# Two-layer block on one core: the SwiGLU input products accumulate in PSUM onto half banks copied by ScalarE, one more pair of column blocks goes by seven products, and half of a gate vector is loaded later

## The chip, the cores and the metric

The kernel runs on one core of a Trainium2 chip. The metric is the device time of one execution in microseconds (us): the median of three runs of the kernel before is 1515.11 us (1514.31 to 1516.73).

## The reference

Two residual layers over 512 tokens of width 1024, all in fp32. Each layer normalizes the tokens, scales and shifts them by conditioning vectors (a SiLU of `c` times a 1024x6144 matrix per layer), applies a mixer (a gated linear recurrence in layer 0, dilated attention in layer 1), adds the result back under a gate, and then does the same with a SwiGLU feed-forward part (FFN):

```python
u = rms_norm(h, norm_g[layer, 2]) * (1.0 + sc2) + sh2
gate, up = jnp.split(u @ w_in, 2, axis=-1)        # w_in: 1024 x 5632
y = (jax.nn.silu(gate) * up) @ w_out              # w_out: 2816 x 1024
h = h + (1.0 + g2) * rms_norm(y, norm_g[layer, 3])
```

The change touches the product `u @ w_in` of both layers and the place at which half of the gate vector `g2` of layer 0 is made.

## The kernel before

**Numbers.** Every fp32 operand of a large product is split into a rounded part and a rest (`hi` and `lo`), and each product is three matmuls: hi by hi, hi by lo, lo by hi (`three`, line 437). ScalarE (ACT) makes the rounded part by a copy with a cast, VectorE (DVE) the rest by a subtraction.

**Weights.** `Stream` (line 38) walks one list of items, written down in order in lines 340 to 425. An item is a 1 MB piece of weights or of a conditioning matrix; two raw buffers hold what has been loaded, SyncE (SP) issues the loads in the order of the list, and a buffer is loaded again when its item has been worked off. `weave` (line 342) puts conditioning items between weight items at a given spacing. A conditioning item is summed on VectorE by four multiply-adds over 512 columns (line 259, its first at line 257), reduced over the partitions on GpSimd (POOL, line 261), and finished by `row_fin` (line 295: two 256 KB rows are loaded and VectorE adds and multiplies, lines 306 and 307) for a gate.

**The first product of an FFN.** `ffn` (line 907) makes 22 blocks of 128 columns for `gate` and as many for `up`. `PLAIN` (line 362) says how many groups of two gate and two up blocks are made directly: per group 4 blocks x 8 slices of the inner dimension x 3 matmuls = 96 matmuls over 512 tokens. The first group is made inside `mixer_out`. The other blocks, two per group, go through `seven_products` (line 771): a gate block and its up block over 512 tokens make a 2x2 by 2x2 block product, and seven smaller products take the place of eight. Each small product (`run`, line 835) is 4 x 3 = 12 matmuls over 256 tokens, so a pair of a gate and an up block takes 84. The left operands are quarters R (three quarters of the weights as they are) and Sm (four sums of quarters); the right operands are quarters of u (`B11`, `B21`, `B22`) and sums of them (`t1`, `t2`, `T3`, `T4`, made once per layer by `token_sums`). `B11` is a copy, shifted by 144 columns.

**The order around the change** is written out by hand (`manual_schedule`): each engine takes its instructions in the program's order. For pair `i`, `runs(i)` puts the seven products into half banks of four PSUM banks (512 fp32 columns each): the four `mm` banks for even pairs, the two `a` and two `b` banks for odd ones. Meanwhile the weights of pair `i+1` are prepared: `r_hi` (ACT, line 802) and `r_lo` (DVE, 806), one sum on GpSimd (`sum_a`, 810), two on VectorE (814, 818), two casts (ACT, 826) and two subtractions (DVE, 830). The seven results of pair `i` are added on the way out of PSUM: two ACT copies of 256 columns (lines 889, 899), VectorE adds (855, 859, 865), a GpSimd add (860), one SiLU (ACT, 866) and the last multiplication (DVE, 870). The tile framework puts the semaphores: whatever two engines do in one PSUM bank is put one after the other, by bank.

**After it**, `y = mid @ w_out` runs per 1 MB weight piece as 48 matmuls over 512 columns. The conditioning items of layer 1 are woven between these pieces.

Of the kernel before, what the change touches and what calls it, by code (L numbers as in the profile page):

```python
# [21 lines left out]
NF = DFF // P  # L22
# [15 lines left out]
class Stream:  # L38
# [120 lines left out]
def block_kernel(tc, x, c, positions, ada_w, ada_b, norm_g, hgrn_w_in, lower, hgrn_norm_g, hgrn_w_out,  # L159
# [8 lines left out]
    with ExitStack() as ctx:  # L168
# [190 lines left out]
        hg.append(win(W, 3 * D + 3 * 256))  # L359
        hg_o = [wtok(hgrn_w_out[0], kq, hf * 512) for hf in range(2) for kq in range(2)]  # L360

        PLAIN = (3, 2)

        def ffn_ws(l):

# [9 lines left out]
        items += weave(hg_o, gate_loads[1:2], 0)  # L375
        f0a, f0b = ffn_ws(0)
        n0 = 2 * PLAIN[0]
        items += weave(f0a[:n0], gate_loads[2:] + [[fin] for fin in gate_fins], 2) + f0a[n0:]
        items += weave(f0b[:9], ada_seq((1, 1), (1, 0)), 0, 0.9) + f0b[9:]
        AW = attn_w_in[0]  # L380

        def av(g, hf):
# [54 lines left out]
        def three(ps, ah, al, bh, bl, start, stop):  # L437
            pe.matmul(ps, ah, bh, start=start, stop=False)  # L438
            pe.matmul(ps, ah, bl, start=False, stop=False)  # L439
            pe.matmul(ps, al, bh, start=False, stop=stop)  # L440
# [327 lines left out]
                    dve.tensor_sub(tl[:, k], t[k], th[:, k].bitcast(F32))  # L768
            return cut

        def seven_products(fs, mid, sgp, spare, th, tl):


            fs = list(fs)
            quarter = lambda a, k: a[:, k * 512:(k + 1) * 512]
# [5 lines left out]
            for copy, t in ((act.copy, uh), (dve.tensor_copy, ul)):  # L781
                for a, b in ((112, 256), (0, 112)):
                    copy(t[:, 0:4, a + 144:b + 144], t[:, 0:4, a:b].bitcast(F32))
            B11 = [(uh[:, k, 144:400], ul[:, k, 144:400]) for k in range(4)]
# [3 lines left out]
            H2 = lambda a: a.rearrange("p (a n) -> p a n", a=2)  # L788
            ring = []
            raw, g_of = {}, {}  # L790
# [12 lines left out]

            def r_lo(i):
                hi, lo = places(i)[0]
                dve.tensor_sub(lo[:, 0:1536], raw[i][:, 512:], hi[:, 0:1536].bitcast(F32))  # L806

            def sum_a(i):
                r = Q4(raw[i])
                pool.tensor_add(r[:, 2], r[:, 2], r[:, 0])  # L810

            def sum_b(i):
                r = Q4(raw[i])
                dve.tensor_tensor(r[:, 0:2], r[:, 0:3:2], r[:, 1:2].broadcast_to((P, 2, 512)), op=OP.add)  # L814

            def sum_c(i):
                r = Q4(raw[i])
                dve.tensor_add(r[:, 3], r[:, 3], r[:, 1])

            def s_cut(i, k):  # L820
                src = Q4(raw[i])[:, 1:3] if k == 0 else Q4(raw[i])[:, 0:4:3]
                return [Q4(t)[:, 2 * k:2 * k + 2] for t in places(i)[1]] + [src]

            def s_hi(i, k):
                hi, lo, src = s_cut(i, k)
                act.copy(hi, src)  # L826
# [12 lines left out]

            def runs(i):  # L840
                R, Sm = places(i)
                b = [bank("mm") for _ in range(4)] if i % 2 == 0 else [bank(t) for t in "abab"]
                g_of[i] = b
                half = lambda n, k: b[n][:, k * 256:k * 256 + 256]
                first = [(half(0, 0), R, 0, B11), (half(3, 1), R, 512, T4), (half(1, 0), R, 1024, B21)]
                for k in (1, 2, 0) if i == 0 else range(3):
                    run(*first[k])
                run(half(1, 1), Sm, 0, t2)
                run(half(2, 1), Sm, 1024, T3)
                run(half(2, 0), Sm, 512, t1)  # L850
                run(half(3, 0), Sm, 1536, B22)

            def sums_1(i):

                dve.tensor_tensor(W[:, 0:5:4], W[:, 2:3].broadcast_to((P, 2, 256)), H2(g_of[i][1]), op=OP.add)

            def sums_2(i):

                dve.tensor_tensor(W[:, 1:6:4], W[:, 4:5].broadcast_to((P, 2, 256)), H2(g_of[i][2]), op=OP.add)
                pool.tensor_add(W[:, 3], W[:, 3], W[:, 5])  # L860

            def sums_3(i):

                if i >= 0:
                    dve.tensor_tensor(W[:, 1:3], W[:, 1:6:4], H2(g_of.pop(i)[3]), op=OP.add)
                    act.activation(W[:, 0:2], W[:, 0:2], AF.Silu)

            def finish(i):
                if i >= 0:
                    dve.scalar_tensor_tensor(H2(mid(fs[i])), W[:, 2:4], -1.0, W[:, 0:2], op0=OP.mult, op1=OP.mult)  # L870

            with tc.manual_schedule(engines=ORDERED):
                r_hi(0)
                r_lo(0)
                sum_a(0)
                sum_b(0)
                sum_c(0)
                for k in range(2):
                    s_hi(0, k)
                    s_lo(0, k)  # L880
                r_hi(1)
                for i in range(len(fs)):
# [5 lines left out]
                    finish(i - 1)  # L888
                    act.copy(W[:, 2], g_of[i][0][:, 0:256])
                    if more:  # L890
                        sum_a(i + 1)
                        sum_b(i + 1)
                        s_hi(i + 1, 0)
                        sum_c(i + 1)
                    sums_1(i)
                    if more:
                        s_lo(i + 1, 0)
                        s_hi(i + 1, 1)
                    act.copy(W[:, 3], g_of[i][2][:, 0:256])
                    if more:  # L900
                        s_lo(i + 1, 1)
                        r_hi(i + 2)
                    sums_2(i)
                sums_3(len(fs) - 1)
                finish(len(fs) - 1)

        def ffn(l, first, close, nxt, side):
            turns.close()
            close()
            with ExitStack() as fx:  # L910
# [4 lines left out]
                with ExitStack() as qx:  # L915
# [6 lines left out]
                    for j in range(PLAIN[l]):  # L922
# [990 lines left out]
```

## Time and profile before

| what | value |
|---|---|
| median of 3 runs | 1515.11 us (1514.31 to 1516.73) |
| the profiled execution, first to last instruction (span) | 1511.0 us |
| TensorE (PE) matmul busy | 1492.8 us, 99% |
| weight loads into TensorE (PEld) | 1308.2 us, 87% |
| VectorE | 1063.6 us, 70% |
| ScalarE | 720.3 us, 48% |
| GpSimd | 234.4 us, 16% |
| granted TensorE clock, mean | 0.997 |
| DMA | 199.14 MB, mean 132 GB/s |

The profile gives no time of its own for the profiled execution besides its span; the median of the timed runs stands 4.1 us above the span. The page's fifth part groups instructions by line, engine and tiles: busy us, mean ns of one, then the engine's idle time ahead of them and who ended it. In the timeline a row is: start, duration, engine, line, operation, output<-inputs, and in brackets the idle time before it and who ended it. Matmuls overlap in it, so the distance from start to start, not the duration, is what one costs.

### The profile page before, as it was taken

How to read it: one execution, taken by the hardware profiler on the slowest of the kernel's cores; microseconds unless marked ns; L12 is line 12 of the kernel's file. 1: busy time of each engine (PE TensorE's matmuls, PEld its weight loads, DVE VectorE, ACT ScalarE, POOL GpSimd, SP SyncE). 2: the span in 40 equal slices, each digit the busy share in tenths (PEclk: the TensorE clock that was granted, in tenths of full speed). 3: DMA queues.
4: the chain of work that ended last, by engine and by line, in shares of the span. 5: the costliest groups of instructions: out<-in, count | busy, mean ns of one | idle time of the engine just before them, and what ended most of it. 6: DMA issues, size and time to landing. Idle time of an engine off the chain costs nothing. (4 is left out here: it accounts for less than half of the span.)

```text
span 1511.0 us, 23542 instructions
## 1 busy us (share of the span) xinstructions
PE 1492.8 (99%) x9231; PEld 1308.2 (87%) x9231; DVE 1063.6 (70%) x1841; ACT 720.3 (48%) x1219; POOL 234.4 (16%) x208
## 2 busy tenths in 40 slices
PE   8999999999999999999999999999999999999998
PEld 6777888898999988888987888988888899999886
DVE  4587867486888896476667766686466978888633
ACT  4433443363454533375545666346655644544231
POOL 1011211031222211140001110011002212221100
PEclk9999999999999999999999999999999999999999
DMA  9654444125333366423166540365213333334521
GB/s 309 183 166 138 156 140 167 56 85 167 113 107 106 105 208 220 155 100 123 57 195 169 150 129 29 113 195 140 84 46 123 98 100 112 109 105 154 209 96 56
DMA packets 206943, 199.14 MB, mean 132 GB/s; under 512 B 6840, under 2 KB 164720, under 8 KB 206576
## 3 DMA queue, kind: packets, MB, share of 16 engines
q1 hardware_dynamic: 203856, 190.87, 40.6%
q10 hardware_dynamic: 1952, 6.65, 1.2%
q8 instruction: 72, 1.18, 0.3%
q0 software_dynamic: 1024, 0.13, 0.2%
q14 instruction: 39, 0.32, 0.1%
HBM read 192.31 MB, written 5.31 MB: 131 GB/s over the span
## 5 line engine op out<-in xcount | busy, mean ns | idle before, releaser
L89 DVE TENSOR_TENSOR lo<-raw,hi 128x2048 fp32r<-128x2048 f32 x68 | 158.8, 2337 | 91.7 <-ACT hi L88 91.7
L88 ACT CAST hi<-raw 128x2048 fp32r<-128x2048 f32 x68 | 129.7, 1908 | 190.3 <-DMA raw<-in_ffn_w_out_dram 55.2
L438 PE MATMUL ps_mm<-apart,hi 128*128 128x512 f32 x384 | 151.4, 394 | 0.0
L439 PE MATMUL ps_mm<-apart,hi 128*128 128x512 f32 x384 | 151.1, 394 | 0.0
L440 PE MATMUL ps_mm<-apart,lo 128*128 128x512 f32 x384 | 150.7, 394 | 0.1
L438 PE MATMUL ps_mm<-uh,hi 128*128 128x512 f32 (+1 forms) x400 | 146.3, 366 | 0.0
L439 PE MATMUL ps_mm<-ul,hi 128*128 128x512 f32 (+1 forms) x400 | 144.3, 361 | 1.0 <-DVE ul L538 1.0
L440 PE MATMUL ps_mm<-uh,lo 128*128 128x512 f32 (+1 forms) x400 | 144.6, 361 | 0.0
L826 ACT CAST hiq<-raw 128x1024 fp32r<-128x1024 f32 x68 | 68.1, 1048 | 64.2 <-DVE raw L814 63.4
L438 PE MATMUL ps_mm<-hi,oh 128*128 128x512 f32 x240 | 94.0, 392 | 0.0
L439 PE MATMUL ps_mm<-lo,oh 128*128 128x512 f32 x240 | 93.4, 389 | 0.0
L438 PEld LDWEIGHTS ps_mm<-uh,hi 128*128 128x128 f32 x400 | 75.5, 189 | 19.7 <-issue 8.4
L439 PEld LDWEIGHTS ps_mm<-ul,hi 128*128 128x128 f32 x400 | 75.6, 189 | 12.1 <-DVE ul L538 1.4
L440 PEld LDWEIGHTS ps_mm<-uh,lo 128*128 128x128 f32 x400 | 75.5, 189 | 11.4
L440 PEld LDWEIGHTS ps_mm<-apart,lo 128*128 128x128 f32 x384 | 72.2, 188 | 15.0 <-DVE lo L89 0.5
L439 PEld LDWEIGHTS ps_mm<-apart,hi 128*128 128x128 f32 x384 | 72.2, 188 | 14.2
L438 PEld LDWEIGHTS ps_mm<-apart,hi 128*128 128x128 f32 x384 | 72.2, 188 | 14.0
L830 DVE TENSOR_TENSOR loq<-raw,hiq 128x1024 fp32r<-128x1024 f32 x68 | 80.0, 1218 | 0.4 <-ACT hiq L826 0.4
L259 DVE SCALAR_TENSOR_TENSOR shared<-raw,cond,shared 128x512 f32<-128x512 f32 x98 | 73.3, 748 | 9.8 <-DMA raw<-in_ada_w_dram 8.8
L261 POOL PARTITION_ALL_REDUCE shared<-shared x14 | 45.9, 3278 | 200.5 <-DVE shared L259 200.5
L810 POOL TENSOR_TENSOR raw<-raw 128x512 f32<-128x512 f32 x34 | 54.7, 1609 | 101.1 <-DVE loq L806 46.3
L440 PE MATMUL ps_mm<-hi,ol 128*128 128x512 f32 x176 | 68.5, 389 | 0.0
(450 smaller groups left out, 4355.2 us busy)
## 6 DMA issues: line engine op xcount, KB each, us to landing
raw<-in_ada_w_dram SPq DMA_DIRECT2D x40, 1024.0 KB, 5.1
raw<-in_ffn_w_in_dram SPq DMA_DIRECT2D x136, 256.0 KB, 3.5
raw<-in_attn_w_in_dram SPq DMA_DIRECT2D x48, 512.0 KB, 5.1
raw<-in_ffn_w_out_dram SPq DMA_DIRECT2D x22, 1024.0 KB, 4.8
raw<-in_hgrn_w_in_dram SPq DMA_DIRECT2D x12, 1024.0 KB, 5.4
raw<-in_attn_w_in_dram SPq DMA_DIRECT2D x12, 1024.0 KB, 4.9
raw<-in_ffn_w_in_dram SPq DMA_DIRECT2D x10, 1024.0 KB, 5.0
first<-in_ada_w_dram SPq DMA_DIRECT2D x14, 512.0 KB, 7.5
```

Of the source, the lines that this page charges most:

```text
L88: self.nc.scalar.copy(hi, t)
L89: self.nc.vector.tensor_sub(lo, t, hi.bitcast(F32))
L259: dve.scalar_tensor_tensor(a, r[:, k], sc, a, op0=OP.mult, op1=OP.add)
L261: pool.partition_all_reduce(a, a, P, bass.bass_isa.ReduceOp.add)
L438: pe.matmul(ps, ah, bh, start=start, stop=False)
L439: pe.matmul(ps, ah, bl, start=False, stop=False)
L440: pe.matmul(ps, al, bh, start=False, stop=stop)
L810: pool.tensor_add(r[:, 2], r[:, 2], r[:, 0])
L826: act.copy(hi, src)
L830: dve.tensor_sub(lo, src, hi.bitcast(F32))
```

## The change

`seven_products` gets three of the four PSUM banks of the last directly made group (`seeded`) and takes one `a` and one `b` bank for itself; a bank's two halves serve even and odd pairs. Instead of adding seven results on VectorE and GpSimd, ScalarE copies a partial sum from one half bank to another inside PSUM, and the next products accumulate onto the copy:

- `first` = B11's product; a copy of it seeds `u2`; then B21's product goes onto `first`, t2's onto `u2`.
- a copy of `u2` seeds `last`; then t1's product goes onto `last`, T4's onto `u2`.
- a copy of `last` seeds `u4`, the other half of `u2`'s bank; then B22's product goes onto `last`.
- `both` = T3's product, copied to SBUF. VectorE adds it to `u2` and `u4` in one instruction and multiplies; the SiLUs of `first` and `last` are two ScalarE instructions.

The first pair uses B11 unshifted, and the shifted copy is made during it. `PLAIN` for layer 0 goes from 3 to 2. Two 1 MB loads of layer 0's `g2` matrix and the finish of that half (two 256 KB rows) go from among the input weights to among the output weights of that FFN, where the spacing of the woven items goes from 0.9 to 0.68.

```diff
-        PLAIN = (3, 2)
+        PLAIN = (2, 2)
...
-        items += weave(f0a[:n0], gate_loads[2:] + [[fin] for fin in gate_fins], 2) + f0a[n0:]
-        items += weave(f0b[:9], ada_seq((1, 1), (1, 0)), 0, 0.9) + f0b[9:]
+        items += weave(f0a[:n0], [[gate_fins[0]]], 2) + f0a[n0:]
+        items += weave(f0b[:9], gate_loads[2:] + [[gate_fins[1]]] + ada_seq((1, 1), (1, 0)), 0, 0.68) + f0b[9:]
...
+            fresh_1, fresh_x = bank("a"), bank("b")
+            class Sums:
+                def __init__(self, i):
+                    p = i % 2
+                    self.first = half(fresh_1, p)
+                    self.both = half(fresh_x, p)
+                    self.pair = seeded[p]
+                    self.u2, self.u4 = half(self.pair, 0), half(self.pair, 1)
+                    self.last = half(seeded[2], p)
...
-            def run(ps, w, o, us):
+            def run(ps, w, o, us, begin):
                 for kt in range(4):
                     a = slice(o + kt * P, o + (kt + 1) * P)
-                    three(ps, w[0][:, a], w[1][:, a], *us[kt], kt == 0, kt == 3)
...
+                    for m, (x, y) in enumerate(((0, 0), (0, 1), (1, 0))):
+                        pe.matmul(ps, w[x][:, a], us[kt][y], start=begin and kt + m == 0, stop=kt == 3 and m == 2,
+                                  skip_group_check=True)
+            def tail_a(i, s):
+                if i >= 0:
+                    act.activation(W[:, 1], s.last, AF.Silu)
+            def tail_b(i, s):
+                if i >= 0:
+                    dve.tensor_tensor(W[:, 2:4], W[:, 4 + i % 2:5 + i % 2].broadcast_to((P, 2, 256)), H2(s.pair), op=OP.add)
+            def tail_c(i):
                 if i >= 0:
                     dve.scalar_tensor_tensor(H2(mid(fs[i])), W[:, 2:4], -1.0, W[:, 0:2], op0=OP.mult, op1=OP.mult)
...
                 for i in range(len(fs)):
                     more = i + 1 < len(fs)
-                    runs(i)
-                    sums_3(i - 1)
...
+                    R, Sm = places(i)
+                    s = Sums(i)
+                    run(s.first, R, 0, B11[i > 0], True)
+                    run(s.both, Sm, 1024, T3, True)
+                    tail_a(i - 1, before)
+                    tail_b(i - 1, before)
+                    act.copy(s.u2, s.first)
+                    tail_c(i - 1)
+                    run(s.u2, Sm, 0, t2, False)
+                    run(s.first, R, 1024, B21, False)
                     if more:
                         r_lo(i + 1)
...
+                        sum_a(i + 1)
+                    act.copy(W[:, 4 + i % 2], s.both)
+                    act.copy(s.last, s.u2)
+                    if i == 0:
+                        shift()
+                    run(s.last, Sm, 512, t1, False)
+                    run(s.u2, R, 512, T4, False)
                     if more:
...
                         sum_b(i + 1)
                         s_hi(i + 1, 0)
                         sum_c(i + 1)
+                        s_hi(i + 1, 1)
                         s_lo(i + 1, 0)
+                    act.copy(s.u4, s.last)
+                    act.activation(W[:, 0], s.first, AF.Silu)
+                    run(s.last, Sm, 1536, B22, False)
                     if more:
                         s_lo(i + 1, 1)
                         r_hi(i + 2)
+                    before = s
+                tail_a(len(fs) - 1, before)
+                tail_b(len(fs) - 1, before)
+                tail_c(len(fs) - 1)
...
-                    seven_products(range(2 * PLAIN[l], NF), mid, sgp, spare, th, tl)
+                    seven_products(range(2 * PLAIN[l], NF), mid, pss, spare, th, tl)
```

More of the change, by code (lines that the diff above doesn't have):

```diff
@@ L769, in token_sums, with seven_products @@
             return cut
-        def seven_products(fs, mid, sgp, spare, th, tl):
+        def seven_products(fs, mid, seeded, spare, th, tl):
             fs = list(fs)
-            quarter = lambda a, k: a[:, k * 512:(k + 1) * 512]
             Q4 = lambda a: a.rearrange("p (s n) -> p s n", s=4)
@@ L779, in seven_products, with shift @@
             B21, B22 = u_of(1, 0), u_of(1, 1)
-            for copy, t in ((act.copy, uh), (dve.tensor_copy, ul)):
+            B11 = [u_of(0, 0), [(uh[:, k, 144:400], ul[:, k, 144:400]) for k in range(4)]]
+            def shift():
                 for a, b in ((112, 256), (0, 112)):
-                    copy(t[:, 0:4, a + 144:b + 144], t[:, 0:4, a:b].bitcast(F32))
-            B11 = [(uh[:, k, 144:400], ul[:, k, 144:400]) for k in range(4)]
+                    for copy, t in ((act.copy, uh), (dve.tensor_copy, ul)):
+                        copy(t[:, 0:4, a + 144:b + 144], t[:, 0:4, a:b].bitcast(F32))
             t1, T3, T4, t2 = (t_of(i) for i in range(4))
@@ L788, in seven_products @@
             H2 = lambda a: a.rearrange("p (a n) -> p a n", a=2)
+            half = lambda b, k: b[:, k * 256:k * 256 + 256]
             ring = []
-            raw, g_of = {}, {}
+            raw = {}
+            fresh_1, fresh_x = bank("a"), bank("b")
[7 more added lines that the diff above has]
+                    self.last = half(seeded[2], p)
             def places(i):
@@ L833, in s_lo @@
                     st.fill()
-            def run(ps, w, o, us):
+            def run(ps, w, o, us, begin):
                 for kt in range(4):
                     a = slice(o + kt * P, o + (kt + 1) * P)
-                    three(ps, w[0][:, a], w[1][:, a], *us[kt], kt == 0, kt == 3)
[L840 to L862, printed above, removed]
-                if i >= 0:
-                    dve.tensor_tensor(W[:, 1:3], W[:, 1:6:4], H2(g_of.pop(i)[3]), op=OP.add)
-                    act.activation(W[:, 0:2], W[:, 0:2], AF.Silu)
-            def finish(i):
+                    for m, (x, y) in enumerate(((0, 0), (0, 1), (1, 0))):
+                        pe.matmul(ps, w[x][:, a], us[kt][y], start=begin and kt + m == 0, stop=kt == 3 and m == 2,
+                                  skip_group_check=True)
+            def tail_a(i, s):
+                if i >= 0:
+                    act.activation(W[:, 1], s.last, AF.Silu)
[3 more added lines that the diff above has]
+            def tail_c(i):
                 if i >= 0:
@@ L881, in seven_products @@
                 r_hi(1)
+                before = None
                 for i in range(len(fs)):
                     more = i + 1 < len(fs)
-                    runs(i)
-                    sums_3(i - 1)
+                    R, Sm = places(i)
[8 more added lines that the diff above has]
+                    run(s.first, R, 1024, B21, False)
                     if more:
                         r_lo(i + 1)
-                    finish(i - 1)
-                    act.copy(W[:, 2], g_of[i][0][:, 0:256])
+                        sum_a(i + 1)
[5 more added lines that the diff above has]
+                    run(s.u2, R, 512, T4, False)
                     if more:
-                        sum_a(i + 1)
                         sum_b(i + 1)
@@ L894, in seven_products @@
                         sum_c(i + 1)
-                    sums_1(i)
-                    if more:
+                        s_hi(i + 1, 1)
                         s_lo(i + 1, 0)
-                        s_hi(i + 1, 1)
-                    act.copy(W[:, 3], g_of[i][2][:, 0:256])
+                    act.copy(s.u4, s.last)
+                    act.activation(W[:, 0], s.first, AF.Silu)
+                    run(s.last, Sm, 1536, B22, False)
                     if more:
@@ L902, in seven_products @@
                         r_hi(i + 2)
-                    sums_2(i)
-                sums_3(len(fs) - 1)
-                finish(len(fs) - 1)
+                    before = s
+                tail_a(len(fs) - 1, before)
+                tail_b(len(fs) - 1, before)
+                tail_c(len(fs) - 1)
         def ffn(l, first, close, nxt, side):
```

## The prediction

> **What bounds the kernel now.** I read the page first, for who is full.
>
> ```profile
> span 1511.0 us, 23542 instructions
> ...
> PE 1492.8 (99%) x9231; PEld 1308.2 (87%) x9231; DVE 1063.6 (70%) x1841; ACT 720.3 (48%) x1219; POOL 234.4 (16%) x208
> ...
> PEclk9999999999999999999999999999999999999999
> ```
>
> PE is busy 99% of the span at a clock that stays at nine tenths or more. Busy time of overlapping matmuls hides small pauses, so next comes the list of what PE waited for. It has eleven rows; the first, the longest, and the only one that names an FFN line:
>
> ```profile
> PE ps_mm L1140 <- DVE late L1135: 2.0, 3, 1.3
> PE ps_mm L1140 <- DVE cols L1170: 1.7, 1, 1.7
> ...
> PE ps_mm L439 <- DVE ul L538: 1.0, 2, 0.5
> ```
>
> That last row (1.0 us, a token split ahead of the FFNs) is no wait of `seven_products`: in both FFNs PE waits for nobody. So time goes only if matmuls go, and comes if PE is made to wait. The stages, by windows: two directly made groups of layer 0, its seven products, and the seven products of layer 1.
>
> ```profile
> core 0: us, PE busy (x) PEld busy (x) DVE busy (x) ACT busy (x) POOL busy (x), PEclk, DMA share, GB/s
> 338.10:381.60 43.50, 43.50 (x194) 36.03 (x193) 32.10 (x30) 15.81 (x16) 4.53 (x2) 1.00 0.48 148
> 381.60:535.40 153.80, 153.80 (x1346) 153.77 (x1345) 131.81 (x146) 73.34 (x94) 35.31 (x31) 1.00 0.40 117
> ...
> 1211.70:1384.60 172.90, 172.90 (x1513) 172.90 (x1512) 144.41 (x158) 82.63 (x106) 38.52 (x33) 1.00 0.38 111
> ```
>
> PE is full in all three, VectorE comes second (131.81 of 153.80 us), ScalarE has half its time free.
>
> **Part 1, one more group by seven products: 2.6 us less.** PE's timeline gives the steps:
>
> ```profile
> 338.08 0.40 PE L438 MATMUL ps_mm<-uh,hi 128*128 128x512 f32 x1
> ...
> 381.63 0.28 PE L438 MATMUL ps_mm<-th,spare 128*128 128x256 f32 x1
> ...
> 391.35 0.28 PE L438 MATMUL ps_a<-uh,hiq 128*128 128x256 f32 x1
> ...
> 525.75 0.28 PE L438 MATMUL ps_a<-uh,hiq 128*128 128x256 f32 x1
> ```
>
> The first row opens the second directly made group, the second ends the third: 2 groups of 96 matmuls in 43.55 us, 21.78 us each, 0.227 us a matmul. The other two are the first matmuls of pairs 1 and 15: 134.40 us for 14 pairs, 9.60 us each, 0.114 us a matmul, 1.37 us a product of 12. A group gives two pairs: 21.78 - 2 x 9.60 = **2.58 us saved**, under the 0.2% (3.0 us) that a measurement of this kernel can tell from no change.
>
> **Part 2, accumulating onto copies: PE waits once in each pair.** PE's order per pair becomes B11, T3, t2, B21, t1, T4, B22. Three of ScalarE's copies stand between a product and one that accumulates on it: `u2` (after B11's product, before t2's; T3's lies between), `last` (after t2's, before t1's; B21's between) and `u4` (after t1's, before B22's; T4's between). What such a copy takes from product to product, by rows:
>
> ```profile
> 389.88 0.28 PE L440 MATMUL ps_mm<-th,loq 128*128 128x256 f32 x1
> 389.99 0.28 PE L438 MATMUL ps_mm<-uh,hiq 128*128 128x256 f32 x1
> ...
> 390.19 0.37 ACT L899 COPY shared<-ps_mm 128x256 f32<-128x256 f32 x1 [1.82 <-PE ps_mm L440]
> ```
> ```profile
> 824.13 0.58 ACT L1809 COPY h<-ps_a 128x512 f32<-128x512 f32 x1
> 824.76 0.30 PEld L1831 LDWEIGHTS ps_b<-h,V 128*128 128x128 f32 x2 [1.77 <-ACT h L1809]
> ```
> ```profile
> 385.78 0.19 PEld L438 LDWEIGHTS ps_mm<-th,hiq 128*128 128x128 f32 x1
> ...
> 385.90 0.29 PE L438 MATMUL ps_mm<-th,hiq 128*128 128x256 f32 x1
> ```
>
> ScalarE's copy starts 0.20 us after the next product has begun (389.99 to 390.19) and takes 0.37; PE's weight load starts 0.05 us after a copy that it waited for (824.71 to 824.76); the matmul follows its weight load by 0.12. Together 0.74 us. Beneath a product of 1.37 us that is hidden, and so it is for `u2` and `last`.
>
> For `u4` it is not. `u4` is the other half of `u2`'s bank, onto which T4's product runs. In the built program this copy does not wait for t1's product: it waits for a count that PE raises only with the last matmul of T4's, because the framework keeps two engines apart by bank. B22's product waits for the copy. So the 0.74 us begin when T4's product ends, and nothing is left on PE to lie over them: the next product in PE's order is the one that waits, and behind it stands the next pair. There are 22 - 4 = 18 pairs in each layer: 36 x 0.74 = **26.6 us added**.
>
> The Trainium skill, "PSUM — Partial Sum Buffer", section "PSUM bank collisions raise a hardware error", speaks against this layout too: it says that two engines must not be in one bank over the same partitions at a time, whichever columns they use, and that PSUM is to be guarded by bank and not by address. No run so far shows such an overlap; by that rule the wait could not be made finer without moving `u4`.
>
> No trace shows ScalarE writing PSUM, so the copy's 0.37 us (PSUM to SBUF) is bounded: the hand-overs alone, 0.37 us, if the copy were free, and the 0.58 us of the row with 512 columns in its place, 0.95. I take 0.37, the row of the same shape. ScalarE's page ("ScalarE: Activation LUTs", section "What happens when an `exp` ACTIVATE runs") in the Trainium skill holds its writes to PSUM faster than those to SBUF, without a number; the sum by it would be somewhat lower.
>
> **Does another chain end later than T4's product?** Before the copy of `u4` ScalarE's order holds both casts of the next pair's sums. Their prices:
>
> ```profile
> L826 ACT CAST hiq<-raw 128x1024 fp32r<-128x1024 f32 x26 | 26.0, 1048 | 25.7 <-DVE raw L814 25.7
> L810 POOL TENSOR_TENSOR raw<-raw 128x512 f32<-128x512 f32 x13 | 21.0, 1616 | 23.1 <-DVE loq L806 12.4 <-DVE spare L806 10.7
> L814 DVE TENSOR_TENSOR raw<-raw 128x1024 f32<-128x1024 f32 x13 | 15.9, 1226 | 15.4 <-POOL raw L810 15.4
> L806 DVE TENSOR_TENSOR spare<-raw,spare 128x1536 fp32r<-128x1536 f32 x6 | 10.5, 1752 | 0.0
> ...
> L870 DVE SCALAR_TENSOR_TENSOR mid<-shared 128x512 f32<-128x512 f32 x13 | 8.9, 684 | 0.0
> ```
>
> From the end of B22's product: SiLU of `last` done at 0.20 + 0.37, last multiplication 0.68, `r_lo` 1.75, GpSimd's sum 1.62, `sum_b` 1.23, two casts 2.10: 7.95 us, some 0.2 more with hand-overs. T4's product ends six products later, at 8.23, and its copy may start at 8.43. The chain has 0.3 us to spare, so it costs nothing; were it longer than I add up, all 36 pairs would pay. VectorE loses two 0.68 us additions a pair and GpSimd one; ScalarE gains about 0.9 us (two copies, and a SiLU in two parts) in half an empty queue. The shifted copy now stands in pair 0 ahead of those casts; PE waits at `u4` there anyway: nothing. B11 unshifted in pair 0 has no row; B21 reads the same columns at 1.36 us, so nothing, at most a product more (1.37) in each layer.
>
> **Part 3, half of `g2` later: nothing.** Two 1 MB loads, two of 256 KB, 8 multiply-adds, 2 finishing steps and one GpSimd reduction leave the directly made groups, where PE was full and stays so, and go behind the first three output weight pieces, past them on SP's queue.
>
> ```profile
> L259 DVE SCALAR_TENSOR_TENSOR shared<-raw,cond,shared 128x512 f32<-128x512 f32 x98 | 73.3, 748 | 9.8 <-DMA raw<-in_ada_w_dram 8.8
> L261 POOL PARTITION_ALL_REDUCE shared<-shared x14 | 45.9, 3278 | 200.5 <-DVE shared L259 200.5
> ```
> ```profile
> 535.40:555.00 19.60, 19.60 (x89) 16.22 (x88) 19.48 (x30) 8.14 (x11) 4.49 (x2) 1.00 0.56 175
> 555.00:575.00 20.00, 20.00 (x90) 16.57 (x89) 15.64 (x36) 6.63 (x8) 3.23 (x1) 1.00 0.68 223
> ...
> 615.00:635.00 20.00, 20.00 (x90) 16.57 (x89) 5.64 (x5) 5.18 (x5) 0.00 (x0) 1.00 0.31 107
> ```
> ```profile
> 552.23 2.28 DVE L89 TENSOR_TENSOR lo<-raw,hi 128x2048 fp32r<-128x2048 f32 x1
> ```
> ```profile
> 608.43 2.29 DVE L89 TENSOR_TENSOR lo<-raw,hi 128x2048 fp32r<-128x2048 f32 x1 [2.78 <-ACT hi L88]
> ```
>
> VectorE takes 8 x 0.75 + 1.4 = 7.4 us more here, and is idle from 615. What matters is when a weight piece is split: the third piece at 554.51, the ninth at 610.72, 9.37 us apart, each with one conditioning item, so 4.7 us an item. PE uses one in 48 x 0.227 = 10.9 us and wants the ninth at 535.4 + 8 x 10.9 = 622.6: a lead of 11.9 us. Two full items and a small one come ahead of it, 9.4 to 14.1 us. So the lead just covers them, and if not, 2.2 us are lost; PE's waits in the stage before add lead (VectorE runs ahead meanwhile). I take nothing.
>
> **Sum.** 1511.0 - 2.6 + 26.6 = 1535.0 us of span. The median of the timed runs stands 4.1 us over that span; kept, that is **1539.1 us**, 1.6% slower.
>
> **The rivals.**
>
> *The copy of `u4` is hidden* (the other side). If it ran beneath T4's product, it would start after the casts, near 8.0 us, and B22's weight load is due at 8.23 - 0.12: PE would lose nothing and only part 1 is left, 1515.1 - 2.6 = 1512.5 us, within 0.2%. It decides at a hand-over of about zero after T4's product. For it: two of the three copies are hidden just so. Against: the built program's wait. Chance 0.04.
>
> *ScalarE's casts end later than T4's product.* The preparing chain (7.95 us and its hand-overs) becomes the period. Half a microsecond over 8.43 would cost 36 x 0.5 = 18 us more: 1557 us. For it: before, GpSimd's sum is what VectorE waits for (15.4 us), and VectorE what the casts wait for (25.7). Against: the sum leaves 0.3 us, and GpSimd loses its other work. Chance 0.05.
>
> *The clock drops.* A pause of 0.74 us in every 10.3 could make the granted clock give way; each tenth lost over both stages costs a tenth of 153.8 + 172.9 + 19.2 us, 35 us: 1574 us. Against it, here PE paused 1.34 us and the clock stayed at 1.00:
>
> ```profile
> 820.00:830.00 10.00, 8.54 (x48) 6.87 (x48) 9.89 (x15) 3.99 (x7) 3.73 (x2) 1.00 0.47 133
> ```
>
> Chance 0.02. The Trainium skill, "TensorE: Matmul & The Clock Gate", section "A second HAM failure mode: psum-queue depth-cycling", reports a kernel whose short pauses between groups of matmuls, while cycling PSUM banks, made the clock go up and down; the row above does not bear that out.
>
> **How the numbers follow.** The forecast has 0.87, the rivals 0.04, 0.05 and 0.02; 0.02 is left for a gain that I don't see. The range comes from the copy's price: 36 x 0.60 - 2.6 gives 1534, and 36 x 0.95 - 2.6 gives 1547; for the copy cheaper than I can bound by the nearest row I go to 1532. Slower by over 0.2%: 0.94; within 0.2%: 0.04; faster: 0.02.
>
> **What would show it.** In the changed profile: PE waits for ScalarE's copy of `u4`, 36 times, near 0.7 us each; pairs 10.3 us apart; no wait at the copies of `u2` and `last`; that copy begins 0.2 us after T4's product; ScalarE idle ahead of it, for PE; no PE wait in the output product of layer 0; clock 1.00. I am wrong if the pairs stay at 9.6 us, or if ScalarE comes to that copy late from its casts.

## The result and the profile after

The changed kernel takes 1536.16 us (median of 4 runs, 1533.8 to 1541.81) against 1514.96 us before: ratio 1.0144, 95% interval 1.0125 to 1.0164, slower. The forecast was 1539.1 us, 1532 to 1547. The profiled execution took 1536.03 us, with a span of 1534.3. Its page, the lines that answer to those of before:

```profile
span 1534.3 us, 23585 instructions
...
PE 1501.6 (98%) x9303; PEld 1313.5 (86%) x9303; DVE 1031.5 (67%) x1783; ACT 751.4 (49%) x1335; POOL 202.6 (13%) x176
...
PEclk9999999999999999999999999999999999999999
```

PE's busy time rose by 8.8 us and the span by 23.3: the rest is idle time of PE. VectorE and GpSimd have 32 us less to do each, ScalarE 31 more. The list of what PE waited for has a new first row, ahead of fourteen others. The three shown below it return later:

```profile
PE ps_mm L856 <- ACT ps_mm L909: 16.0, 36, 0.4
...
PE ps_b L1844 <- ACT h L1822: 1.1, 2, 0.8
...
PE ps_b L1853 <- ACT h L1822: 0.5, 1, 0.5
...
PE ps_mm L439 <- DVE lo L89: 0.4, 1, 0.4
```

L856 is the matmul in `run`, L909 the copy of `u4`: 36 waits, one in each pair of both layers, and none for another copy. The list gives 16.0 us, 0.45 each. PE's timeline shows that it is more. First the two first matmuls of B22's product in consecutive pairs, then the last matmul of T4's in one pair and what follows it, with the weight load and ScalarE's rows at that place:

```profile
389.22 0.39 PE L856 MATMUL ps_mm<-uh,hiq 128*128 128x256 f32 x1 [0.45 <-ACT ps_mm L909]
```
```profile
399.54 0.39 PE L856 MATMUL ps_mm<-uh,hiq 128*128 128x256 f32 x1 [0.45 <-ACT ps_mm L909]
```
```profile
429.80 0.28 PE L856 MATMUL ps_mm<-th,spare 128*128 128x256 f32 x1
430.52 0.39 PE L856 MATMUL ps_mm<-uh,hiq 128*128 128x256 f32 x1 [0.45 <-ACT ps_mm L909]
430.75 0.28 PE L856 MATMUL ps_mm<-ul,hiq 128*128 128x256 f32 x1
```
```profile
430.52 0.19 PEld L856 LDWEIGHTS ps_mm<-uh,hiq 128*128 128x128 f32 x1 [0.64 <-ACT ps_mm L909]
```
```profile
430.11 0.36 ACT L909 COPY ps_mm<-ps_mm 128x256 f32<-128x256 f32 x1 [0.66 <-PE ps_mm L856]
430.38 0.39 ACT L910 ACTIVATE shared<-ps_a 128x256 f32<-128x256 f32 x1
```

Pairs are 10.32 to 10.33 us apart, where the forecast had 9.60 + 0.74. From the last matmul of T4's product to the first of B22's are 0.72 us where 0.114 is the rule, so 0.61 is lost there. The next step is 0.23 instead of 0.114, so 0.11 more: 0.72 us a pair, and 0.725 by the distances (10.325 less 9.60). The list of waits counts from a modelled end of the last matmul (430.08) and leaves out both the restart and the part of 0.28 us that matmuls usually overlap. The distance from start to start is what counts. 36 times 0.725 is 26.1 us; less 2.6 for the direct group, 23.5, and the spans differ by 23.3.

### The profile page after: what moved, and what is told of

Read it like the earlier page. It is cut to its first block, busy times and chain, and to the rows that moved or that the text cites. A ratio compares the mean times of both kernels' runs of the same rounds, so it can differ in the third digit from the quotient of the medians.

```text
span 1534.3 us, 23585 instructions
## 1 busy us (share of the span) xinstructions
PE 1501.6 (98%) x9303; PEld 1313.5 (86%) x9303; DVE 1031.5 (67%) x1783; ACT 751.4 (49%) x1335; POOL 202.6 (13%) x176
## 5 line engine op out<-in xcount | busy, mean ns | idle before, releaser
L439 PE MATMUL ps_mm<-apart,hi 128*128 128x512 f32 x384 | 151.2, 394 | 0.0
L438 PE MATMUL ps_mm<-uh,hi 128*128 128x512 f32 (+1 forms) x368 | 133.9, 364 | 0.0
L439 PE MATMUL ps_mm<-ul,hi 128*128 128x512 f32 (+1 forms) x368 | 131.9, 358 | 1.0 <-DVE ul L538 1.0
L440 PE MATMUL ps_mm<-uh,lo 128*128 128x512 f32 (+1 forms) x368 | 132.2, 359 | 0.0
L856 PE MATMUL ps_mm<-th,hiq 128*128 128x256 f32 x360 | 99.4, 276 | 0.0
L856 PE MATMUL ps_mm<-tl,hiq 128*128 128x256 f32 x360 | 99.4, 276 | 0.0
L856 PE MATMUL ps_mm<-th,loq 128*128 128x256 f32 x360 | 99.4, 276 | 0.0
L847 DVE TENSOR_TENSOR loq<-raw,hiq 128x1024 fp32r<-128x1024 f32 x72 | 85.1, 1222 | 18.7 <-ACT hiq L843 18.7
L827 POOL TENSOR_TENSOR raw<-raw 128x512 f32<-128x512 f32 x36 | 48.2, 1339 | 356.8 <-DVE loq L823 170.6
L439 PE MATMUL ps_mm<-lo,oh 128*128 128x512 f32 x240 | 93.6, 390 | 0.4 <-DVE lo L89 0.4
L438 PEld LDWEIGHTS ps_mm<-uh,hi 128*128 128x128 f32 x368 | 69.5, 189 | 18.5 <-issue 8.4
L439 PEld LDWEIGHTS ps_mm<-apart,hi 128*128 128x128 f32 x384 | 72.2, 188 | 14.2
L439 PEld LDWEIGHTS ps_mm<-ul,hi 128*128 128x128 f32 x368 | 69.6, 189 | 10.8 <-DVE ul L538 1.4
```

The costliest lines, as they stand in the source:

```text
L856: pe.matmul(ps, w[x][:, a], us[kt][y], start=begin and kt + m == 0, stop=kt == 3 and m == 2, skip_group_check=True)
```

## The experiments

Each ratio is to the kernel before on the same chip. "Pairs" are the distances between pairs in the timeline.

**1. `u4` in a bank of its own.** The direct groups' fourth bank is free during the seven products.

```
-                    self.pair = seeded[p]
-                    self.u2, self.u4 = half(self.pair, 0), half(self.pair, 1)
+                    self.u2, self.u4 = half(seeded[p], 0), half(seeded[3], p)
...
-                    dve.tensor_tensor(W[:, 2:4], W[:, 4 + i % 2:5 + i % 2].broadcast_to((P, 2, 256)), H2(s.pair), op=OP.add)
+                    for k, u in ((2, s.u2), (3, s.u4)):
+                        dve.tensor_add(W[:, k], W[:, 4 + i % 2], u)
```

> The changed kernel with `u4` in the fourth bank that the direct groups leave free, so that no copy shares a bank with the product that runs while it is due; the addition of `both` becomes two of 256 columns. Theory (the copy of `u4` waits for T4's product because both are in one bank, and nothing covers its 0.72 us): the copy runs beneath T4's product, PE waits nowhere in the seven products, pairs 9.60 us apart, 1536.2 - 36 x 0.72 = 1510 us, at most 1513. Rival A (accumulating onto a half that ScalarE wrote costs PE by itself): the pairs stay near 10.3 us and the time near 1536. Rival B (ScalarE's casts come late to that copy): the copy starts when the casts end, not when a product ends; some 1515 to 1530, with PE waits of changing length.

Measured: 1517.79 us, ratio 1.0020 (1.0007 to 1.0033). PE's list of waits has no row of the seven products. The timeline of this kernel (its matmul line is L855; the first matmuls of two consecutive pairs, then the end of T4's and the start of B22's product, then ScalarE and B22's first weight load at that place):

```profile
439.59 0.28 PE L855 MATMUL ps_a<-uh,spare 128*128 128x256 f32 x1
```
```profile
449.19 0.28 PE L855 MATMUL ps_a<-uh,hiq 128*128 128x256 f32 x1
```
```profile
438.12 0.28 PE L855 MATMUL ps_mm<-th,loq 128*128 128x256 f32 x1
438.23 0.28 PE L855 MATMUL ps_mm<-uh,hiq 128*128 128x256 f32 x1
```
```profile
435.77 2.00 ACT L842 CAST hiq<-raw 128x1024 fp32r<-128x1024 f32 x2 [1.01 <-DVE raw L830]
437.67 0.37 ACT L909 COPY ps_mm<-ps_mm 128x256 f32<-128x256 f32 x1
```
```profile
438.12 0.19 PEld L855 LDWEIGHTS ps_mm<-uh,hiq 128*128 128x128 f32 x1
```

9.60 us a pair, 0.11 from T4's last matmul to B22's first. The bank of `u4` makes the difference between the two kinds of pairs; rival A falls. (The edit also splits one addition of VectorE into two; the second try of 2 comes to the same pairs without that.) The copy now begins beneath T4's product, when the casts end (437.67), and ends at 438.04, 0.08 us ahead of B22's weight load at 438.12. So the shared bank hid a second bound of nearly the same length, as the prediction's chain had it. The total is 5 us above the 1513 that were the most expected; see 5 and 6.

**2. The same banks in another order.** B22's product goes behind the next pair's first, T3's behind t2's, B21's behind t1's, T4's last:

```
+                    if i:
+                        run(before.last, *late, B22, False)
...
                     run(s.u2, Sm, 0, t2, False)
...
+                    if i:
+                        run(s.both, Sm, 1024, T3, True)
...
                     run(s.last, Sm, 512, t1, False)
+                    run(s.first, R, 1024, B21, False)
+                    act.copy(s.u4, s.last)
...
+                    run(s.u2, R, 512, T4, False)
```

> All banks as in the changed kernel; only the order is another: B22's product of a pair comes after the first product of the next pair, T3's after t2's, B21's after t1's, T4's last, and the copy of `u4` is issued ahead of T4's product. Each of the three copies then has a product in another bank between its source and its reader. Theory: no wait, pairs 9.60 us apart except the first of each layer (one uncovered copy, 0.7 us each), 1511 us, at most 1514. Rival A (accumulating onto copies costs by itself): near 1536. Rival C (the shared bank is bad wherever the copy stands, because it must still wait for the bank): waits move to T4's product, 1520 to 1536.

Measured: 1567.98 us, ratio 1.0334 (1.0313 to 1.0355), 11.03 us a pair: none of the theories. PE's waits, then VectorE's rows in one pair:

```profile
PE ps_a L856 <- ACT shared L914: 37.1, 32, 1.4
```
```profile
438.81 0.69 DVE L869 SCALAR_TENSOR_TENSOR mid<-shared 128x512 f32<-128x512 f32 x1 [1.82 <-ACT shared L861]
439.42 1.75 DVE L823 TENSOR_TENSOR spare<-raw,spare 128x1536 fp32r<-128x1536 f32 x1
```

No wait at `u4` is left, but another is there: the next pair's first product waits for the SiLU of `first` (L914). The `first` of two neighbouring pairs are the two halves of one bank, so this wait, too, is one by bank. With B22 a product later, the SiLU of `last` came later, VectorE's last multiplication (L869) waited 1.82 us for it, and behind that stood `r_lo` (L823), the head of the chain to the casts and that SiLU. I had moved a product without following what stands behind its readers. The second try puts `r_lo` ahead of the multiplication and the copy of `u4` between the casts:

```
                     tail_b(i - 1, before)
+                    if more:
+                        r_lo(i + 1)
+                        sum_a(i + 1)
                     act.copy(s.u2, s.first)
...
+                        s_hi(i + 1, 0)
+                        sum_c(i + 1)
+                    act.copy(s.u4, s.last)
+                    if more:
+                        s_hi(i + 1, 1)
```

> The changed kernel's banks with the order in which every copy has a product of another bank between its source and its reader, and now with VectorE's remainder `r_lo` ahead of its last multiplication, and ScalarE's copy of `u4` between the two casts, since in the first try the SiLU of `first` came 1.4 us late behind that chain and the next pair's first product waited for it. Theory: 9.60 us a pair but for the first of each layer, 1511 to 1518. If the chain is still the longer one: PE waits for that SiLU again, 10 to 11 us a pair, 1525 to 1560.

Measured: 1512.76 us, ratio 0.9997 (0.9986 to 1.0009). Pairs 9.60 us. Of the seven products only two waits are left, one in each layer's first pair:

```profile
PE ps_mm L856 <- ACT ps_mm L899: 0.9, 2, 0.4
```

So the shared bank does no harm in itself. What counts is that a product of another bank lies between the copy and its neighbours.

**3. The copy ahead of T4's product; the SiLU ahead of the copy.**

```
+                    act.copy(s.u4, s.last)
                     run(s.u2, R, 512, T4, False)
...
-                    act.copy(s.u4, s.last)
```

> The changed kernel with one line moved: the copy of `u4` is issued ahead of T4's product, directly behind t1's. Theory: the same 0.72 us of hand-over now lie between t1's product and T4's, with nothing on PE between them either; PE waits at T4's product instead of B22's, pairs 10.3 us apart, 1536 us (1534 to 1539). If it were the sharing of the bank alone that costs, whatever the order, the wait would go with the order: 1510 us.

Measured: 1546.67 us, ratio 1.0214 (1.0194 to 1.0234). The wait went to T4's product, and is as long:

```profile
PE ps_mm L856 <- ACT ps_mm L902: 17.9, 36, 0.5
```

Pairs are 10.38 to 10.49 us, up to 0.16 longer than in the changed kernel, 4 us in all; why a pause there costs a little more was not found. Of the other 6 us some 3 lie at the start of the two output products, where PE now waits for a cast (`oh`, 2.6 us by the list of waits, no such row in the changed kernel); the rest lies in the attention (6).

```
-                    act.copy(s.u4, s.last)
                     act.activation(W[:, 0], s.first, AF.Silu)
+                    act.copy(s.u4, s.last)
```

> The changed kernel with two neighbouring ScalarE lines swapped: the SiLU of `first` (0.39 us) comes ahead of the copy of `u4`. Theory: ScalarE stands idle for 0.83 us ahead of that copy, waiting for T4's product, so the SiLU fits there and nothing changes: 1536 us, within 2. Rival B (ScalarE's own chain ends late and sets the copy's start): 36 x 0.27 to 0.39 us more, 1546 to 1550.

Measured: 1544.28 us, ratio 1.0191 (1.0177 to 1.0206). By its total it speaks for rival B, by its trace it doesn't: pairs 10.34 us, against 10.33. The copy's own view, in this kernel and in the changed one, has these rows; the two after the heading tell ScalarE's idle time ahead of the copy:

```profile
its engine sat idle before it (us, times) until:
  PE ps_mm L856: 17.6, 35
```
```profile
its engine sat idle before it (us, times) until:
  PE ps_mm L856: 29.8, 36
```

The SiLU used up part of an idle time of 0.83 us, and the copy still starts when PE lets it. ScalarE's chain did not set the pause. The total's 8 us lie outside the FFNs (6).

**4. The copy done twice.**

```
                     act.copy(s.u4, s.last)
+                    act.copy(s.u4, s.last)
```

> The changed kernel with the copy of `u4` done twice, the second time writing the same numbers. Theory (whatever ScalarE does between T4's product and B22's is paid in full): ScalarE's next instruction starts 0.27 us after the copy, so each pair is 0.27 us longer, 10.60 us; 36 x 0.27 = 9.7 us more, some 1546 (1543 to 1549). If the pause were a fixed cost of the hand-over between the engines, and not of the copy: 10.33 us a pair, 1536.

Measured: 1557.66 us, ratio 1.0278 (1.0256 to 1.0300). ScalarE's rows and two starts of B22's product:

```profile
433.24 0.36 ACT L909 COPY ps_mm<-ps_mm 128x256 f32<-128x256 f32 x1 [0.67 <-PE ps_mm L856]
433.62 0.36 ACT L910 COPY ps_mm<-ps_mm 128x256 f32<-128x256 f32 x1
```
```profile
434.03 0.39 PE L856 MATMUL ps_mm<-uh,hiq 128*128 128x256 f32 x1 [0.83 <-ACT ps_mm L910]
```
```profile
444.80 0.39 PE L856 MATMUL ps_mm<-uh,hiq 128*128 128x256 f32 x1 [0.83 <-ACT ps_mm L910]
```

10.77 us a pair, 0.44 more, not 0.27: the second copy, to the same half, starts 0.39 us behind the first, where the SiLU to another place starts 0.27 behind. So ScalarE's time between T4's and B22's products is paid in full, and the price was misjudged. The list of waits has 34 of these and not 36: in the last pair of each layer the built program runs B22's product among the first matmuls of the output product, an order that the kernel does not write down. 34 x 0.44 = 15.0 us of the 21.5 over the changed kernel. The rest lies behind the seven products: PE waits at the start of both output products (`oh`, 0.98 us each), once for `lo` in the first of them (1.62 us), and longer in the attention (6).

**5. The parts taken apart.** The changed kernel again:

> The changed kernel once more, unaltered, beside the others of this set, since the parts outside the seven products differed by several us among the profiles so far. If those parts differ from execution to execution, the pairs stay 10.33 us apart and the total moves by some us: 1533 to 1543. If the first reading was typical, 1536 within 1.5.

Measured: 1536.93 us, ratio 1.0151 (1.0133 to 1.0170), pairs 10.33 us: the first reading was typical. The old products with the other two parts of the change:

```
-        PLAIN = (3, 2)
+        PLAIN = (2, 2)
...
-        items += weave(f0a[:n0], gate_loads[2:] + [[fin] for fin in gate_fins], 2) + f0a[n0:]
-        items += weave(f0b[:9], ada_seq((1, 1), (1, 0)), 0, 0.9) + f0b[9:]
+        items += weave(f0a[:n0], [[gate_fins[0]]], 2) + f0a[n0:]
+        items += weave(f0b[:9], gate_loads[2:] + [[gate_fins[1]]] + ada_seq((1, 1), (1, 0)), 0, 0.68) + f0b[9:]
```

> The products, sums and copies of the kernel before, with only the other two parts of the change: one direct group fewer in layer 0 (18 pairs there), and half of the conditioning vector's loads later. Theory (these two are worth 21.78 - 2 x 9.60 = 2.6 us and nothing else): 1512.6 us, PE waits nowhere in the FFNs but perhaps 0.4 us in layer 0's output product. Rival D (the moved loads or the missing group cost what the kernel with `u4` in its own bank lost against its forecast, some 5 us): 1516 to 1519.

Measured: 1513.33 us, ratio 0.9999 (0.9988 to 1.0011). The 2.6 us aren't in the total. The new sums with `u4` in its own bank, three direct groups and the old loads (the same lines the other way):

> `u4` in its own bank, but with three direct groups in layer 0 and the loads where they were before: only the sums of products are new. Theory (the new sums cost PE nothing once no copy is waited for; the direct group and the loads are all that is left): 9.60 us a pair, 1515.2 us, as before. Rival D: 1515 too. Rival E (the new sums, by ScalarE's or VectorE's other work, cost the 5 us that were missing): 1518 to 1521.

Measured: 1511.78 us, ratio 0.9983 (0.9974 to 0.9992), below what either theory gave. The new sums cost nothing and seem to gain 2.6 us, and not within the products, where the pairs are 9.60 us apart as before. The two profiles' waits outside the FFNs add up to 11.3 us before and 8.3 here. Why was not tried.

Then, from the kernel of 1, the moved loads with three groups, and two groups with the loads as before; and that kernel once more:

```
-        PLAIN = (2, 2)
+        PLAIN = (3, 2)
```

> `u4` in its own bank, three direct groups in layer 0 as before, but the conditioning loads moved as in the change. Differs from the kernel at 1511.8 us only by the loads, and from `u4` in its own bank with two groups only by the group. Theory F (the moved loads cost the 5 us that were missing there: with them a late weight piece stops PE for 0.5 to 3.8 us at the end of layer 1's attention in every profile so far): 1514 to 1517. Theory G (the group's removal brings them): 1512.

```
-        items += weave(f0a[:n0], [[gate_fins[0]]], 2) + f0a[n0:]
+        items += weave(f0a[:n0], gate_loads[2:] + [[fin] for fin in gate_fins], 2) + f0a[n0:]
-        items += weave(f0b[:9], gate_loads[2:] + [[gate_fins[1]]] + ada_seq((1, 1), (1, 0)), 0, 0.68) + f0b[9:]
+        items += weave(f0b[:9], ada_seq((1, 1), (1, 0)), 0, 0.9) + f0b[9:]
```

> `u4` in its own bank, two direct groups in layer 0, but the conditioning loads woven into the direct groups as before. Theory F (the moved loads cost): 1511.8 - 2.6 = 1509, faster than both kernels by some 5 us, if VectorE still gets its conditioning items done beside two groups. Theory G (fewer groups shift the later stages against the loads): 1514 to 1518, with a PE wait near the end of the attention.

> `u4` in its own bank, all else as in the change, once more on the same chip as the two variants of its loads and groups. If the loss outside the FFNs is the kernel's: 1515 to 1518 again, at or above the kernel before. If it came from that chip: 1512 to 1513.

Measured: 1514.91 us, ratio 0.9990 (0.9981 to 0.9998), for the late loads; 1525.49 us, 1.0063 (1.0047 to 1.0079), for the early ones; 1515.55 us, 0.9994 (0.9982 to 1.0006), for the kernel of 1 once more. So theory F is wrong: late loads cost no 5 us, and early ones, with two groups, cost 10 more than late ones. Theory G is no better: on this chip the kernel of 1 lost nothing against the kernel before, so part of the first reading's 5 us didn't come back (6 says which). The early ones' PE waits in the first pair of layer 0:

```profile
PE ps_b L855 <- ACT hiq L842: 2.5, 1, 2.5
...
PE ps_a L855 <- ACT spare L818: 1.8, 1, 1.8
...
PE ps_a L855 <- DVE spare L822: 1.3, 1, 1.3
...
PE ps_b L855 <- DVE loq L846: 0.7, 1, 0.7
```

They add up to 6.3 us: with two groups and the conditioning items still among them, VectorE and ScalarE don't get the first pair's weights ready. From just behind the first of these pauses the granted TensorE clock is at half for 10.2 us (PEclk, the number after the last pair of brackets):

```profile
362.80:373.00 10.20, 6.23 (x25) 5.64 (x26) 7.94 (x8) 4.01 (x5) 2.45 (x2) 0.50 0.29 84
```

PE worked for 6.23 of these 10.2 us, at 0.21 us a matmul of 256 columns instead of 0.114, so some 3 us more are lost. With the 6.3 that is most of the 10. The profiled execution was the shortest of the six; four of the others had a lower mean clock (0.991 to 0.993, against 0.995). The moved loads, a part that the prediction counted at nothing, are what the removed group needs.

Is the group's 2.6 us there at all? The kernel of 1 (second profile) and the one with three groups, both with late loads: a wait ahead of the FFN and the first matmul of layer 0's output product behind it, in the one and in the other:

```profile
314.55 0.39 PE L439 MATMUL ps_mm<-ul,hi 128*128 128x256 f32 x1 [0.47 <-DVE ul L538]
```
```profile
533.63 0.40 PE L438 MATMUL ps_mm<-hi,oh 128*128 128x512 f32 x1
```
```profile
313.74 0.39 PE L439 MATMUL ps_mm<-ul,hi 128*128 128x256 f32 x1 [0.47 <-DVE ul L538]
```
```profile
535.35 0.40 PE L438 MATMUL ps_mm<-hi,oh 128*128 128x512 f32 x1
```

219.08 against 221.61 us: 2.53 us are saved there, and are not in the totals (0.9994 against 0.9990).

**6. Where they went, and the stray 5 us.** They went into the attention behind. PE's waits at the two products that take ScalarE's transposed copies (L1844, L1853) in the kernel of 1 (second profile), then with three groups and late loads:

```profile
PE ps_b L1853 <- ACT h L1822: 2.8, 1, 2.8
PE ps_b L1844 <- ACT h L1822: 2.8, 3, 2.2
```
```profile
PE ps_b L1844 <- ACT h L1822: 1.4, 2, 1.0
...
PE ps_b L1853 <- ACT h L1822: 0.7, 1, 0.7
```

5.6 against 2.1 us. In the eleven profiles with two groups in layer 0 these two waits add up to 1.6 to 6.1 us, 1.6 and 2.8 in the two of the unaltered change; in the three with three groups 1.0 to 2.1. In the kernel of 1 (first profile) the copy is late because a cast ahead of it on ScalarE waited for a weight load:

```profile
1031.68 1.91 ACT L88 CAST hi<-raw 128x2048 fp32r<-128x2048 f32 x1 [4.92 <-DMA raw<-in_attn_w_in_dram]
```

With three groups and the old loads the same cast waited 2.85 us. So the removed group's gain is met by longer waits in the attention behind, and in the profile shown that wait begins with a late load. These waits differ from kernel to kernel by as much as the gain, most kernels were profiled once, and why the loads land later stays open. The stray us of 1 and 3 stand there too: from the last B22 product of layer 0 to the first of layer 1 PE takes 687 us in the changed kernel, and 689, 692 and 694 in those of 1, the copy ahead (with the wait for `oh`) and the SiLU ahead.

The waits are not all of it: behind a long one the granted TensorE clock falls. In the first profile of the kernel of 1 PE's wait of 2.64 us at L1853 ends at 1036.58; what follows is too short to show in the page's row of tenths, which has nine in every slice:

```profile
1036.90:1040.30 3.40, 3.40 (x16) 3.21 (x15) 1.77 (x12) 0.88 (x2) 0.00 (x0) 0.50 0.96 271
```

For 3.4 us the clock is at half. Two matmuls of L1853 take 0.43 us from start to start there, 0.22 in the changed kernel, so some 1.7 us are lost. Such a stretch follows all six of the waits at these two products that are longer than 2.4 us, two of the nine of 1.5 to 2.4 us, and none of the shorter ones; one more follows a wait of 1.78 us at another product. All nine stand in kernels with two groups: one in the first profile of the kernel of 1, two in the second, none in the changed kernel's two, and none in the three profiles with three groups. That the wait brings the lower clock is read from the order of the two, and was not tried.

With that the first profile of 1 can be accounted for. Its span is 3.2 us above that of before, where 2.6 less were expected: 5.8 us. The waits outside the seven products are 2.1 us longer (13.4 against 11.3), the stretch at half clock in the attention costs some 1.7, and one at the start of the kernel, before any changed line, is 3.4 us longer than before the change (6.8 against 3.4), some 1.7 again. This last part has nothing to do with the change: the second profile of the changed kernel has no such stretch at its start.

## Why the prediction was right

- **What bounds the kernel.** Right: in the changed kernel time came only from PE being made to wait.
- **Part 1, 2.58 us saved.** Right in its place: 2.53 us, and the changed kernel's span has it (23.5 us by the sum, 23.3 measured). That is in part luck: of the eleven profiles with two groups this one has the shortest waits in the attention (1.6 us), and no stretch at half clock there. With no wait for `u4`, two groups are no faster than three (0.9994 and 0.9990). This step of the sum stopped at the end of the FFN; it didn't ask which later wait would take the time back.
- **Part 2, 36 x 0.74 us.** Right: 0.72 to 0.73, and the pieces too. The copy starts 0.31 us after T4's last matmul starts (0.11 + 0.20 forecast), takes 0.36 (0.37), the weight load comes 0.05 after it (0.05), and the matmuls are in step 0.11 later (0.12; the first matmul starts with its weight load, at 430.52, and the second comes 0.11 late). That the bank causes it was argued from the built program, and is shown by 1, 2 and 3: another bank, or another product in between, removes it; another place for the copy moves it. The Trainium skill ("PSUM — Partial Sum Buffer", "PSUM bank collisions raise a hardware error") has PSUM guarded by bank; the overlap itself wasn't tried, and the runs agree in that another bank lets the copy run beside T4's matmuls. What the Trainium skill says in "ScalarE: Activation LUTs" on faster writes to PSUM (it stands in the section "Step-by-step: what each stage is for", not in the one that the prediction names) is borne out, by little: the copy of `u4` takes 0.357 us in the changed kernel and 0.368 in that of 1, against 0.373 for the same shape to SBUF.
- **The other chain.** Right that it comes earlier, too careful with 0.3 us: ScalarE stood idle for 0.83 us ahead of the copy. GpSimd's sum was priced at 1.62 us from before; beside another order of VectorE's work it takes 1.29 in the stretch shown, 1.34 over the whole run:

```profile
L827 POOL TENSOR_TENSOR raw<-raw 128x512 f32<-128x512 f32 x15 | 19.3, 1287 | 135.6 <-DVE loq L823 72.3 <-DVE spare L823 54.2 <-DMA raw<-in_ffn_w_in_dram 9.0
```

- **Part 3, nothing.** Nearly right for the path that I followed: one wait of 0.4 us in layer 0's output product (L439 on `lo`, at 633.87), where up to 2.2 was feared. It missed what the move is for (5: 6.3 us of waits, and a lower clock among them, if it is left out).
- **The rivals.** The hidden copy didn't come, and it is what 1 built. There it needs the casts to end 0.08 us in time. Had that chain been 0.1 us longer, it would be the next bound. The clock stayed at 1.00 through the 36 pauses of 0.72 us. The row is layer 0's; layer 1's shows 1.00 as well:

```profile
362.24:548.00 185.76, 177.74 (x1501) 173.78 (x1500) 126.64 (x129) 99.90 (x165) 20.74 (x17) 1.00 0.36 104
```

  The row that the prediction held against this rival (a pause of 1.34 us at 1.00) is shorter than any wait that a lower clock followed (6). The changed kernel's pauses drew none; longer waits in some of its variants were followed by one.

- **The sum.** 2.9 us too high. 0.5 of it is the pause (26.6 against 26.1). The rest is in the step from span to median: 4.1 us were kept, because that was the difference before; the profiled execution took 1.7 us longer than its span (1536.03 and 1534.3). In every execution on record the time is some 1.7 us above the span, so the profiled execution before, with a span of 1511.0, took some 1512.7 us: it was 2.4 us faster than the median, and this was carried over.

## What to carry to other kernels

When an engine other than PE writes into PSUM between two products, look at which product PE runs meanwhile, and in which bank: the copy is free beneath a product in a third bank, and costs the whole round trip (here 0.72 us for 256 columns) where the neighbour in PE's order is in the copy's own bank or is its reader. Reckon a pause from start to start of matmuls, not from the list of waits, which showed 0.45 of the 0.72. And a few us saved in one stage count only when the stages behind it are seen to keep them: here later waits took them back, and the lower clock that follows the longest of them.

## What the runs showed of the hardware

- After a pause the first two matmuls start 0.22 to 0.23 us apart instead of 0.114, and the first lasts 0.39 us instead of 0.28: a restart costs PE about 0.11 us beyond the wait.
- Two ScalarE copies to the same half of a bank start 0.39 us apart, a copy and a SiLU to different places 0.27. Whether the engine or the built program holds the second back was not separated.
- Accumulating matmuls onto numbers that ScalarE wrote into a bank cost the same as onto a product: 9.60 us a pair either way.
- The granted clock fell to half, for 3.4 us each time, behind all six waits of PE of 2.6 to 3.9 us in the attention and behind two of the nine of 1.5 to 2.4 us. It stayed at full through 36 pauses of 0.72 us, and through 32 waits of 1.1 to 1.4 us, one in every 11 us (the first try of 2).
